# The first layer's adaLN weights: five buffers, and their pool nested inside the norm's

## The chip, the cores and the metric

The kernel runs on one core of a Trainium2 chip. The metric is the device time of one execution in microseconds (us), the median of several runs.

## The reference, cut to what matters

Two layers of a hybrid backbone run over 128 context tokens and 1024 latent tokens, model width 1024, all in float32. Both groups share one set of weights. Each sub-layer is normalised, shifted, scaled and gated by values that come from a conditioning vector (adaLN):

```
mod_p = (silu(c_ctx) @ ada_w[l] + ada_b[l]).reshape(-1, 1, 6, 1024)
mod_s = (silu(c)     @ ada_w[l] + ada_b[l]).reshape(-1, 1, 6, 1024)
hp = modulate(rms_norm(yp, norm_g[l, 0]), mod_p, 0)
hs = modulate(rms_norm(ys, norm_g[l, 0]), mod_s, 0)
# layer 0: even_mixer(h)
q, ff, fb, i, g, hy = split_cols(h @ w_in, (512, 512, 512, 512, 512, 1536))
o_a = bidir_scan(...)                        # HGRN2, 4 heads
hy = dwconv3(hy, hy_conv_w, hy_conv_b);  v, x1, x2 = split(hy, 3)
filt = hyena_filters(L, w1, b1, w2, b2, w3, freq)   # sin, sin, linear, window
z = v
for o, gate in enumerate((x1, x2)):
    z = gate * (two_sided_fftconv(z, filt[o]) + z * hy_d[o])
out = concat([head_rms(o_a) * silu(g), z]) @ w_out
```

After it come a gated ConvFFN, and layer 1 (differential attention and gated linear attention) with another ConvFFN.

## The kernel before

The tokens are nine tiles of 128 rows (one of context, eight latent). A scheduler sets the order of the instructions on each engine ahead of the run: PE (TensorE), DVE (VectorE), ACT (ScalarE), POOL (GpSimd) and SP, which issues nearly all transfers. Each engine works through its order and waits where an instruction's input or buffer is not ready. Every float32 product of the large matrices is three matmuls of a high and a low part (`mm3`, L203 to L207), so each weight is split after its load: the high part on ACT (L211), the low part on DVE or POOL (L218).

What stands at the start of layer 0, in `run`:

- `filter_mlp` (L729): two sine layers over the positions of the Hyena filter; a matmul (L748), seven steps on DVE (L750 to L756), a sine on ACT (L758), three times each layer.
- `ada` (L372), here for group 0, the first four of the twelve blocks of 512 columns: eight loads of 1 MB (`adaw`, L382), four matmuls for each into the PSUM bank tagged `g` (L384), then bias and gain on DVE (L399, L400), four transposes (L408) and copies into `modc`. With `bufs=3` the fourth load waits for the first buffer.
- `first_norm` (L448): for each token tile a load into one of four buffers `y` (L451), square and scale on ACT (L426, L431), and in `to_hT` for each of two half tiles four transposes (L439), the modulation on DVE into one of two buffers `f` (L442), the high part on ACT (L445, `hTh`) and the low part on POOL (L218, `hTl`).
- `filter_tables` (L767) splits the tables of the Fourier transform (`traw`, `tqh`, `tql`), and `columns` (L307) turns small vectors into columns (`rows`, L331, L334, L336).
- `filter_spectra` (L781): the spectra of the filters. The last linear layer's weights are loaded into `X` (L796), summed on POOL (L798) and split (`w3h` on ACT, `w3l` on POOL); matmuls of 256 columns (L812, tag `h`), a window from memory (`win`, L819) multiplied on DVE (L814), a split (`fh` on ACT, `fl` on POOL) and matmuls tagged `f`.
- `hy_in` (L603): the projection of the Hyena columns, twelve blocks of 128 columns, matmuls of 388 columns tagged `g`. Its weights come through `weights` (L225): one load buffer `wraw` (L233) and three each of `whi` and `wlo`, in the pool `gw`.

Then `hyena` (L882), the HGRN projection `hgrn_in` (L645) and the scans of four heads (`hgrn`, L663, `scan`, L485; tags `b` and `c`), beside which the adaLN weights of the other rows are loaded.

Pools on a side of the memory are stacked: a pool opened after others were closed begins where they began, and each tile in it waits until the earlier tiles on its bytes are done. On the left side lie `hT`, then the pools `ada` (weights) and `fn` (norm), and after these two are closed `gw` and `hi` (projection); on the right `keep`, `fm`, and above them first `ml` and `ms` (sine layers) and then `fs` (spectra).

Of the kernel before, what the change touches and what calls it, by code (L numbers as in the profile page):

```python
# [31 lines left out]
def drain(gen):  # L32
    for _ in gen:
        pass
# [160 lines left out]
class Kern:  # L195
# [1273 lines left out]
    def run(self):  # L1469
        L, R = "left", "right"  # L1470
# [4 lines left out]
        with ExitStack() as es:  # L1475
# [6 lines left out]
            with self.psum(g=2, t=2, f=2, h=2):  # L1482
                with self.urgent():
                    self.setup(es)
                self.open_hT(e_hT)
                with self.pool("ada", 1) as ap, self.pool("fn", 2) as np_:
                    with self.pool("ml", 1, R) as mp, self.pool("ms", 2, R) as ms:
                        with self.urgent():
                            self.filter_mlp(keep, mp, ms)
                            drain(self.ada(0, ap, (0,), 3, "g", "t"))  # L1490
                            self.first_norm(np_)
                        self.filter_tables(fp, ms)
                        self.columns()
                    fs = e_keep.enter_context(self.pool("fs", 2, R))
                    drain(self.filter_spectra(fp, fs))
                gw = es_gw.enter_context(self.pool("gw", 3))
                hio = es_hi.enter_context(self.pool("hi", 2))
                drain(self.hy_in(gw, hio, range(4)))
# [58 lines left out]
            with self.psum(b=2, s=4, w=1, ad=1), self.pool("wo", 2) as wo, self.pool("ada", 1) as ad, \  # L1557
# [3 lines left out]
                t = al.tile([P, P], F32, name="p3")  # L1561
# [65 lines left out]
```

## Time and profile before

| | us |
|---|---|
| median of three runs | 3528.32 |
| lowest and highest of the three | 3524.34, 3535.78 |
| the profiled execution | 3525.83 |
| its span, first to last instruction | 3523.8 |

The profile is of one execution. The page gives each engine's busy time and the span in 40 slices; the views of the trace give busy time in chosen stretches, groups of instructions by line, and the instructions in order of time with what ended the idle time before them. PE and PEld are TensorE's matmuls and weight loads; the granted clock is a share of 2.4 GHz.

### The profile page before, as it was taken

The page shows a single profiled execution, that of the slowest core. Times are in us where ns is not written, and L with a number is a line of the kernel's source. Part 1 is how long each engine was busy: PE and PEld are TensorE (multiplying, and loading weights), DVE is VectorE, ACT ScalarE, POOL GpSimd, SP SyncE. Part 2 cuts the span into 40 slices and gives each one's busy share as a digit, 9 for nine tenths or more (in the row PEclk, how much of TensorE's full clock was granted, in tenths as well). Part 3 has the DMA queues.
Part 4 walks back from the last instruction along what each step waited for, and adds up shares of the span by engine and source line. Part 5 has one row for each costly group of instructions (what it writes and reads, how often), then busy time and mean ns, then how long its engine had stood idle before and what let it go on. Part 6 is the DMA issues. An engine that isn't in the chain of part 4 may idle for free.

```text
span 3523.8 us, 55879 instructions
## 1 busy us (share of the span) xinstructions
PE 3334.1 (95%) x23022; PEld 3024.4 (86%) x23022; DVE 1880.8 (53%) x3342; ACT 1354.2 (38%) x2414; POOL 876.4 (25%) x596
## 2 busy tenths in 40 slices
PE   5999999888899999999999999989988999999998
PEld 2999999756699999999988998857767999999997
DVE  5658987488653333433372247558786233343334
ACT  5334333453443222232264334346565322232223
POOL 2432230001442222332240003211125222232214
PEclk7999999999899999999999999989998999999999
DMA  6445334483421110111143323484123110111114
GB/s 217 135 149 151 119 103 136 161 290 123 161 68 48 37 42 25 54 48 43 36 148 119 133 79 115 127 276 108 41 93 104 44 41 26 49 49 48 37 30 138
DMA packets 272701, 348.09 MB, mean 99 GB/s; under 512 B 14354, under 2 KB 231597, under 8 KB 266302
## 3 DMA queue, kind: packets, MB, share of 16 engines
q1 hardware_dynamic: 269294, 334.82, 30.1%
q0 software_dynamic: 3152, 9.70, 0.9%
q8 instruction: 181, 2.97, 0.4%
q14 instruction: 74, 0.61, 0.1%
HBM read 266.58 MB, written 77.89 MB: 98 GB/s over the span
## 4 chain that ended last, share of the span: by engine, by line
PE 79%; DVE 7%; DMA 5%; ACT 3%; issue 3%; POOL 2%; SPq 0%; POOLq 0%; ACTq 0%; DVEq 0%
PE g L206 9%; PE g L207 9%; PE g L205 9%; PE a L205 7%; PE a L206 7%; PE a L207 7%; PE d L205 5%; PE d L206 5%; PE d L207 5%; DMA adaw<-in_ada_w 2%; PE b L1344 1%; PE s L1328 1%; DVE f L442 1%; DVE acc L1002 1%; PE w L205 1%
## 5 line engine op out<-in xcount | busy, mean ns | idle before, releaser
L206 PE MATMUL g<-hTl,whi 128*128 128x388 f32 (+2 forms) x1728 | 589.1, 341 | 2.3 <-POOL hTl L218 2.3
L205 PE MATMUL g<-hTh,whi 128*128 128x388 f32 (+2 forms) x1728 | 588.9, 341 | 2.3 <-ACT hTh L445 2.3
L207 PE MATMUL g<-hTh,wlo 128*128 128x388 f32 (+2 forms) x1728 | 587.6, 341 | 0.0
L206 PE MATMUL a<-hTl,whi 128*128 128x388 f32 (+2 forms) x1248 | 426.7, 342 | 2.6 <-POOL hTl L218 2.6
L205 PE MATMUL a<-hTh,whi 128*128 128x388 f32 (+2 forms) x1248 | 426.9, 342 | 1.4 <-ACT hTh L445 1.4
L207 PE MATMUL a<-hTh,wlo 128*128 128x388 f32 (+2 forms) x1248 | 423.3, 341 | 0.0
L1002 DVE TENSOR_TENSOR acc<-d,acc 128x512 f32<-128x512 f32 x288 | 197.8, 688 | 334.4 <-PE d L207 333.0
L1104 POOL TENSOR_TENSOR ta<-ta,tg 128x386 f32<-128x386 f32 x132 | 135.6, 1027 | 918.2 <-ACT tg L1103 884.0
L205 PEld LDWEIGHTS g<-hTh,whi 128*128 128x128 f32 x1728 | 326.8, 189 | 6.7 <-ACT hTh L445 2.9
L206 PEld LDWEIGHTS g<-hTl,whi 128*128 128x128 f32 x1728 | 326.4, 189 | 6.7 <-POOL hTl L218 2.9
L207 PEld LDWEIGHTS g<-hTh,wlo 128*128 128x128 f32 x1728 | 326.2, 189 | 2.0
L205 PE MATMUL d<-dh,ah 128*128 128x512 f32 x792 | 312.4, 395 | 1.2 <-DVE acc L1002 1.2
L207 PE MATMUL d<-dh,al 128*128 128x512 f32 x792 | 311.8, 394 | 0.0
L206 PE MATMUL d<-dl,ah 128*128 128x512 f32 x792 | 311.7, 394 | 0.0
L476 ACT ACTIVATE tg<-g,cols,cols 128x386 f32<-128x386 f32 x132 | 88.9, 673 | 499.7 <-PE g L207 499.4
L218 POOL TENSOR_TENSOR wlo<-wraw,whi 128x1024 fp32r<-128x1024 f32 x90 | 217.1, 2413 | 165.7 <-ACT whi L211 165.2
L218 POOL TENSOR_TENSOR dl<-draw,dh 128x1024 fp32r<-128x1024 f32 x60 | 147.8, 2464 | 398.8 <-ACT dh L211 327.4
L205 PEld LDWEIGHTS a<-hTh,whi 128*128 128x128 f32 x1248 | 236.5, 189 | 10.2 <-issue 2.2
L206 PEld LDWEIGHTS a<-hTl,whi 128*128 128x128 f32 x1248 | 236.3, 189 | 9.7 <-POOL hTl L218 3.6
L477 DVE SCALAR_TENSOR_TENSOR tg<-g,cols,tg 128x386 f32<-128x386 f32 x132 | 81.8, 620 | 296.6 <-ACT tg L476 296.6
L207 PEld LDWEIGHTS a<-hTh,wlo 128*128 128x128 f32 x1248 | 236.3, 189 | 4.1 <-issue 1.6
L211 ACT ACTIVATE whi<-wraw 128x1024 fp32r<-128x1024 f32 x145 | 152.7, 1053 | 180.0 <-DMA wraw<-in_ffn_up 66.6
(429 smaller groups left out, 7047.7 us busy)
## 6 DMA issues: line engine op xcount, KB each, us to landing
adaw<-in_ada_w SPq DMA_DIRECT2D x48, 1024.0 KB
wraw<-in_ffn_up SPq DMA_DIRECT2D x88, 512.0 KB
draw<-in_ffn_down SPq DMA_DIRECT2D x44, 512.0 KB
wraw<-in_w_in_even SPq DMA_DIRECT2D x32, 512.0 KB
wraw<-in_w_in_odd SPq DMA_DIRECT2D x24, 512.0 KB
hgT<-po SPq DMA_DIRECT2D x16, 576.0 KB
ymid<-acc SPq DMA_DIRECT2D x18, 512.0 KB
y<-ymid SPq DMA_DIRECT2D x18, 512.0 KB
```

Of the source, the lines that this page charges most:

```text
L205: mm(out, lh, rh, start=start, stop=False)
L206: mm(out, lh, rl, start=False, stop=False)
L207: mm(out, ll, rh, start=False, stop=stop)
L211: eng.activation(out, in_, AF.Copy)
L218: eng.tensor_tensor(out, a, b, ALU.subtract)
L442: nc.vector.tensor_scalar(f[:, j], pt[:, 128 * j:128 * j + 128], mod[:, 1, g, k:k + 1], mod[:, 0, g, k:k + 1], ALU.mult, ALU.add)
L476: nc.scalar.activation(out, ps[:, 1:1 + n], AF.Identity, scale=w[1], bias=b)
L477: nc.vector.scalar_tensor_tensor(out, ps[:, 0:n], w[0], out, ALU.mult, ALU.add)
L1002: nc.vector.tensor_tensor(acc[:, i, s], ps, acc[:, i, s], ALU.add)
L1104: nc.gpsimd.tensor_tensor(ta, ta, tg, ALU.mult)
L1328: nc.tensor.matmul(s[:, k0:k0 + 512], q[:, p, 128 * t:128 * t + 128], kx[:, p, k0:k0 + 512], start=(x == 0), stop=(x == 1))
L1344: nc.tensor.matmul(po, w[:, c], v[:, c], start=(c == 0), stop=(c == NT - 1))
```

## The change

The pool `ada` moves inside the block in which `ml` and `ms` are open, and is opened after `fn` in place of before it; it closes before `fs` is opened. The adaLN weights of group 0 get five buffers in place of three.

```diff
-                with self.pool("ada", 1) as ap, self.pool("fn", 2) as np_:
-                    with self.pool("ml", 1, R) as mp, self.pool("ms", 2, R) as ms:
+                with self.pool("fn", 2) as np_:
+                    with self.pool("ada", 1) as ap, self.pool("ml", 1, R) as mp, self.pool("ms", 2, R) as ms:
                         with self.urgent():
                             self.filter_mlp(keep, mp, ms)
-                            drain(self.ada(0, ap, (0,), 3, "g", "t"))
+                            drain(self.ada(0, ap, (0,), 5, "g", "t"))
                             self.first_norm(np_)
                         self.filter_tables(fp, ms)
                         self.columns()
```

The scheduler sets other orders from it. On SP, at the start, the loads before (`adaw` are the adaLN weights, `y` the token tiles, `traw` tables, `rows` small vectors):

```order
L382 DMA adaw<-in_ada_w 128x2048 x3
L451 DMA y<-in_x_prompt 128x1024
L451 DMA y<-in_x_sample 128x1024 x3
L774 DMA traw<-in_const_dft_q 128x1024 x2
L331 DMA rows<-in_hgrn_lb 24x128
L331 DMA rows<-in_hgrn_norm 4x128
L331 DMA rows<-in_hy_conv_w 36x128
L331 DMA rows<-in_hy_conv_b 12x128
L382 DMA adaw<-in_ada_w 128x2048
L394 DMA adab<-in_ada_b 2x512 x3
L396 DMA adag<-in_norm_g 2x512
L394 DMA adab<-in_ada_b 2x512
```

and now:

```order
L382 DMA adaw<-in_ada_w 128x2048 x5
L451 DMA y<-in_x_prompt 128x1024
L451 DMA y<-in_x_sample 128x1024 x3
L774 DMA traw<-in_const_dft_q 128x1024 x2
L331 DMA rows<-in_hgrn_lb 24x128
L331 DMA rows<-in_hgrn_norm 4x128
L382 DMA adaw<-in_ada_w 128x2048
L394 DMA adab<-in_ada_b 2x512 x3
L396 DMA adag<-in_norm_g 2x512
L394 DMA adab<-in_ada_b 2x512
L396 DMA adag<-in_norm_g 2x512
L382 DMA adaw<-in_ada_w 128x2048
```

Two more weight loads go ahead of the token tiles, and the sixth to eighth come ahead of the third and fourth table.

Further on in SP's order, where the projection's weights (`wraw`) are first loaded, before:

```order
L777 DMA traw<-in_const_dft_p 128x256
L331 DMA rows<-in_ffn_conv_w 44x128
L331 DMA rows<-in_ffn_conv_b 44x128
L233 DMA wraw<-in_w_in_even 128x8x128
L451 DMA y<-in_x_sample 128x1024 x2
L233 DMA wraw<-in_w_in_even 128x8x128
L451 DMA y<-in_x_sample 128x1024 x2
L233 DMA wraw<-in_w_in_even 128x8x128
L796 DMA X<-in_hy_w 64x1024 x2
L819 DMA win<-in_const_hy_win 128x2x256
```

and now (`X` are the weights of the spectra, `win` their windows):

```order
L777 DMA traw<-in_const_dft_p 128x256
L331 DMA rows<-in_ffn_conv_b 44x128
L451 DMA y<-in_x_sample 128x1024 x5
L796 DMA X<-in_hy_w 64x1024 x2
L819 DMA win<-in_const_hy_win 128x2x256
L825 DMA at_721<-in_hy_d 1x256
L819 DMA win<-in_const_hy_win 128x2x256 x2
L233 DMA wraw<-in_w_in_even 128x8x128
L825 DMA at_869<-in_hy_d 1x256
L819 DMA win<-in_const_hy_win 128x2x256
```

The first load of projection weights has moved behind the last five token tiles, the spectra's weights and three windows.

On PE, from the transposes of the adaLN rows (L408) to the first projection matmuls (`g<-hTh,whi`), before:

```order
L408 MATMUL t<-ident,adab 128x128
L439 MATMUL t<-ident,y 128x128 x4
L408 MATMUL t<-ident,adab 128x128 x3
L748 MATMUL f<-sh_211,hw_143 64x384
L439 MATMUL t<-ident,y 128x128 x32
L205 MATMUL g<-hTh,whi 128x388
L206 MATMUL g<-hTl,whi 128x388
L207 MATMUL g<-hTh,wlo 128x388
```

and now, first the transposes:

```order
L408 MATMUL t<-ident,adab 128x128
L439 MATMUL t<-ident,y 128x128 x4
L408 MATMUL t<-ident,adab 128x128 x3
L439 MATMUL t<-ident,y 128x128 x4
L748 MATMUL f<-sh_185,hw_143 64x384
L748 MATMUL f<-hz,hw_141 64x384
L439 MATMUL t<-ident,y 128x128 x24
L748 MATMUL f<-sh_211,hw_143 64x384
L439 MATMUL t<-ident,y 128x128 x40
L812 MATMUL h<-w3h,hs 128x256
L812 MATMUL h<-w3h,hs 32x256
```

and then the place where the projection begins:

```order
L205 MATMUL f<-fh,tqh 128x256
L206 MATMUL f<-fl,tqh 128x256
L207 MATMUL f<-fh,tql 128x256
L812 MATMUL h<-w3h,hs 128x256
L812 MATMUL h<-w3l,hs 128x256
L205 MATMUL g<-hTh,whi 128x388
L206 MATMUL g<-hTl,whi 128x388
```

The transposes of the norm (L439) now all stand ahead of the projection, and so do the first matmuls of the spectra (L812 and `f`).

## Rows read from the trace of the kernel before

**Rows 1.** The page, part 2: PE busy in 40 slices of 88 us, in tenths.

```profile
PE   5999999888899999999999999989988999999998
```

**Rows 2.** Stretches: length, busy us (count) of PE, PEld, DVE, ACT, POOL; clock, DMA, GB/s.

```profile
0.00:42.00 42.00, 19.52 (x69) 3.52 (x69) 14.62 (x42) 20.60 (x31) 5.38 (x16) 1.00 0.85 316
42.00:92.00 50.00, 29.32 (x122) 20.53 (x121) 35.67 (x105) 31.66 (x49) 21.71 (x17) 0.62 0.45 122
92.00:350.00 258.00, 256.98 (x1761) 256.13 (x1759) 165.80 (x288) 107.29 (x197) 83.58 (x76) 1.00 0.48 145
681.00:694.00 13.00, 3.91 (x111) 3.27 (x111) 6.75 (x7) 6.17 (x9) 0.00 (x0) 0.61 1.00 342
694.00:840.00 146.00, 131.58 (x1868) 87.22 (x1869) 116.03 (x174) 74.22 (x118) 13.16 (x14) 0.95 0.73 255
840.00:1000.00 160.00, 131.69 (x1004) 107.61 (x1004) 119.40 (x236) 75.90 (x136) 60.30 (x30) 0.86 0.36 117
```

**Rows 3.** Groups by line, PE, 0 to 91.9 us: count, busy us, mean ns, idle.

```profile
L205 PE MATMUL g<-hTh,whi 128*128 128x388 f32 x9 | 4.3, 482 | 2.3 <-ACT hTh L445 2.3
L206 PE MATMUL g<-hTl,whi 128*128 128x388 f32 x8 | 3.9, 490 | 2.3 <-POOL hTl L218 2.3
L207 PE MATMUL g<-hTh,wlo 128*128 128x388 f32 x8 | 3.6, 456 | 0.0
L812 PE MATMUL h<-w3h,hs 128*128 128x256 f32 (+1 forms) x7 | 1.9, 314 | 1.8 <-ACT w3h L211 1.8
L812 PE MATMUL h<-w3l,hs 128*128 128x256 f32 (+1 forms) x7 | 1.9, 317 | 0.0
```

**Rows 4.** In order of time, to 45 us, ACT, PE, SP: start, us, what, idle.

```profile
15.66 1.06 ACT L426 ACTIVATE junk<-y 128x1024 bf16<-128x1024 f32 x1 [12.06 <-DMA y<-in_x_prompt]
25.31 1.94 PE L384 MATMUL g<-adaw,csx 128*32 128x512 f32 x8 [7.44 <-DMA adaw<-in_ada_w]
32.77 1.93 PE L384 MATMUL g<-adaw,csx 128*32 128x512 f32 x8
34.77 0.33 SPq L382 DMA_DIRECT2D adaw<-in_ada_w  x1
42.12 1.89 PE L384 MATMUL g<-adaw,csx 128*32 128x512 f32 x8
```

**Rows 5.** DMA, 0 to 45 us, in 40 slices of 1.1 us: rate.

```profile
GB/s 0 57 154 233 430 394 336 336 323 270 277 397 419 422 422 419 411 429 423 407 269 168 226 430 308 284 422 390 419 452 430 357 204 415 354 98 0 0 0 7
```

**Rows 6.** In order of time, 51 to 101 us, the norm on DVE, ACT, POOL.

```profile
51.58 1.36 DVE L442 TENSOR_SCALAR f<-t,modc 128x128 f32<-128x128 f32 x4
52.98 0.64 ACT L445 ACTIVATE hTh<-f 128x512 fp32r<-128x512 f32 x1 [2.29 <-DVE f L442]
53.77 1.09 POOL L218 TENSOR_TENSOR hTl<-f,hTh 128x512 fp32r<-128x512 f32 x1 [47.20 <-ACT hTh L445]
73.10 1.36 DVE L442 TENSOR_SCALAR f<-t,modc 128x128 f32<-128x128 f32 x4 [0.24 <-POOL hTl L218]
81.91 1.36 DVE L442 TENSOR_SCALAR f<-t,modc 128x128 f32<-128x128 f32 x4 [7.38 <-POOL hTl L218]
98.02 2.64 DVE L442 TENSOR_SCALAR f<-t,modc 128x128 f32<-128x128 f32 x8 [0.36 <-POOL hTl L218]
```

**Rows 7.** In order of time, 63 to 93 us, projection weights and spectra weights.

```profile
63.35 1.04 ACT L211 ACTIVATE whi<-wraw 128x1024 fp32r<-128x1024 f32 x1
71.95 0.69 PE L205 MATMUL g<-hTh,whi 128*128 128x388 f32 x1 [2.27 <-ACT hTh L445]
76.00 1.28 POOL L798 TENSOR_TENSOR X<-X 128x512 f32<-128x512 f32 x1 [2.94 <-DMA X<-in_hy_w]
82.87 2.38 POOL L218 TENSOR_TENSOR w3l<-X,w3h 128x1024 fp32r<-128x1024 f32 x1
92.42 0.34 PE L205 MATMUL g<-hTh,whi 128*128 128x388 f32 x1
92.60 0.34 PE L206 MATMUL g<-hTl,whi 128*128 128x388 f32 x1
```

## The prediction

> **What bounds the kernel now.** I read the page's slices first, then the stretches, then the start in order of time. The only slice in which TensorE (PE) has a digit under 8 is the first [rows 1]: the front is where loads and buffers can matter, and all that follows moves with the moment at which PE is filled for good. The stretches say when that is: 19.5 us of PE work in the first 42 us, 29.3 us in the next 50 us at a mean granted clock of 0.62, then 257.0 of 258 us at full clock [rows 2]. So the front can be put in one number: **the moment at which PE is filled, less the projection and spectra work that it has already done by then**. By 91.9 us it has done 25 matmuls of the first projection (tag g) and 14 of the spectra (tag h) [rows 3]. At full clock one g matmul follows the other after 0.18 us (92.42, 92.60 [rows 7]), so 25 are 4.5 us; an h matmul has 256 columns in place of 388, so some 0.12 us, and 14 are 1.7 us. The front of the kernel before ends, so counted, at 92.0 - 6.2 = 85.8 us. The next stretches with gaps in PE are the scans, 694 to 1000 us: 131.6 of 146 and 131.7 of 160 us busy, with DVE at 116.0 and 119.4 us [rows 2].
>
> **Term 1, five buffers.** With three buffers the eighth weight load is issued at 34.77 us, when the matmuls of the fifth weight, which began at 32.77, have given their buffer back; the last matmuls start at 42.12 [rows 4]. So one buffer wait is real. But the transfers are near their limit anyhow: in the first 42 us the DMA share is 0.85 at a mean of 316 GB/s [rows 2], which is 13.3 MB, and the loads in that stretch (eight weights of 1 MB, four token tiles and four tables of 0.5 MB) are 12.6 MB. Five buffers change the order in which these bytes come, not their number. Two more weights go ahead of the first token tiles, so the prompt rows, whose square starts at 15.66 us [rows 4], come later by 2.1 MB / 316 GB/s, some 6 us. The eighth weight lands after 11.5 MB instead of 12.6, at 3 + 36 = 39 us by the mean rate, and at 3 + 27 = 30 us by the 420 GB/s of the better slices [rows 5]. In the changed order its matmuls stand behind the second sine layer, which waits for the first sine on ACT; and in ACT's order the sine stands behind the scaling of the token tiles, which come 6 us later. So I put the last weight matmuls at 39 to 41 us. From their end, 44.0 us before, DVE needed until 51.58 [rows 4, 6] to modulate the first half tile (L442), with sine steps and table splits in between; these stand there still, more of them. I take 50 for the first L442. Bounds: no gain (51.6), and 6 us of gain, if DVE has done these by then.
>
> The Trainium skill, page "DMA: Bandwidth & Descriptors", section Specifications, puts the HBM limit of one core at some 358 GB/s; by that the eighth weight lands no sooner than 3 + 32 = 35 us. The trace agrees in its mean, 316 GB/s, not in its slices of 1.1 us, which go to 420 GB/s and over [rows 5]. The Trainium skill, page "Perfetto Trace Analysis", section Optimization Strategy, says that the same gap coming again on an engine can mean too few buffers; by that rule PE's waits for the weights would go, which is the second rival below.
>
> **Term 2, the nesting: what the projection's weights lie on.** This is the larger part. Pools on one side are stacked. Before, the adaLN weights' pool stood below the norm's, and the ring of the projection weights (gw), opened when both are closed, began on the adaLN weights, done with at 44 us. Now the norm's pool stands below, so the ring begins on the norm's token buffers and statistics, in use until the ninth token tile is transposed. The orders show it: the first load of projection weights stood on SP ahead of the fifth token tile, and now stands behind all nine, behind the spectra's weights and three windows; on PE all 72 transposes of the norm now stand ahead of the first g matmul. Before, g began at 71.95 [rows 7]. What that costs:
> - The norm's 18 half tiles. The first nine took (73.10 - 51.58) / 8 = 2.7 us each; then DVE stood 7.38 us until POOL, which had waited for the spectra's weights and done their sums and a weight split, gave a buffer free; the last nine, 81.91 to 99.4 us, took 2.2 us each [rows 6, 7]. Now no projection weight is split among them (three on ACT, two on DVE, one on POOL are gone from there), and POOL does fourteen half tiles before the spectra's sums. I take 2.2, of the undisturbed half. Bounds: DVE's own 1.36 [rows 6], which no row comes near, and 2.7.
> - From 50 us the fourteenth half starts at 50 + 13 x 2.2 = 78.6; with DVE 1.36, ACT 0.64 and POOL 1.09 [rows 6] it is out at 81.7. Then POOL: two sums (2 x 1.28), two half tiles (2.2), the low part of the spectra's weights (2.38): 88.8 us, against 82.87 + 2.38 = 85.3 before [rows 7].
> - The first spectra product on DVE, some 0.7 us later, frees a window buffer; behind it SP issues the first projection weights, at some 90.5. Their 0.5 MB need at least 1.7 us at the mean rate, and less than the 7.3 us that 1 MB needed from 34.77 to 42.12 at most [rows 4]; I take 3.7. The split's first half is 1.04 [rows 7]: g starts at some 95.2.
> - By then PE has done some 20 h and 18 f matmuls, 38 x 0.12 = 4.6 us. The front ends at 95.2 - 4.6 = 90.6, against 85.8: **5 us lost**. PE also starts this work from the lower clock level, 1.2 GHz, to which it falls while it only transposes (mean 0.62 of full from 42 to 92 us [rows 2]); before it had risen by 92. That is up to 2 us more, left to the range.
>
> **Term 3, behind the front.** PE's work is the same in sum. The orders differ up to the end of the HGRN scans and are the same behind. One difference has a sign: the spectra now run ahead of the projection, so the Hyena stage and the first scan begin earlier in PE's order. When the first scan's matmuls (tag b) begin, 265 g matmuls are still to come, before 216: 49 x 0.18 = 8.8 us of head start. From 694 us on two scans share DVE, which is busy 0.79 and 0.75 of the time [rows 2]. The scans on the left cannot begin before the last g matmul, because their buffers lie on the projection's inputs, so the gap of 681 to 694, 9.1 us of idle PE [rows 2], stays. What the head start gives is the scan work done before 681. Between nothing and 8.8 us I take **3 us won**, since a scan alone mostly waits for its own chain.
>
> **Sum.** +5 - 3 = +2 us. Against the profiled execution (3525.83 us, its span 3523.8) that is 3527.8; the median of the three runs shown, 3528.32, is 2.5 us above that execution, so I forecast 3530 us. A measurement of this kernel can tell about 0.3%, 10.6 us, from no change: the band is 3517.7 to 3538.9.
>
> **Rivals.**
> 1. *Slower: the half tiles stay at 2.7 us.* The norm's chain through PE, DVE, ACT and POOL with two buffers is then the bound, not the weights' splits between. For it: the first nine took 2.7 with two projection weights among them, and the new ACT order has six changes of its function table in the norm, before three. Against: the last nine took 2.2 beside spectra work. The fourteenth half then starts at 85.1, 6.5 us later, and the projection with it: +11.5; the scans give nothing back if DVE is what they wait for; with a part of the clock's 2 us that is 3528.3 + 13 = 3541. It decides from 2.6 us per half tile on. Chance 0.2.
> 2. *Faster: the buffers do what they are for.* If PE's waits for weights (7.44 us the longest [rows 4]) go and DVE is free when the last one is done, the norm starts at 45.6 in place of 50; with POOL and ACT free of projection weights it runs at 1.9, and 13 halves save 3.9. Then +5 - 4.4 - 3.9 - 3 = -6, and with the whole head start -12: 3516. Against: the DMA share of 0.85. Chance 0.12.
> 3. *The loss is paid back.* The front loses its 5 us, the scans give all 8.8: -4, 3524.5, no difference that can be told. That five buffers do nothing at all, because the bytes set the pace, ends in the forecast or here. Chance 0.13.
>
> **How the numbers follow.** The forecast has 0.55 and lies within the band, rival 3 too: same 0.68. Rival 1 is slower, 0.2; rival 2 faster, 0.12. The range reaches from rival 2 (3516, less 2 for the run-to-run spread) to rival 1 with all of the clock's 2 us and the same spread: 3514 to 3545.
>
> **What would show it.** Right: the last weight matmuls near 40 us and the first L442 near 50; no g matmul before 90 us; POOL without a long stop in the norm; the low part of the spectra's weights done near 88; PE filled from 94 to 96 us on, and the scans' stretch, 306 us before, some us shorter. Wrong: a first L442 before 46, half tiles at 2.7 or under 2, a g matmul before 85, or a change of the scans' stretch of over 8 us either way, which would be an effect of the new order that I have given no price.

## The result and the profile after

The changed kernel takes 3552.7 us (median of four runs, 3548.9 to 3555.6) where the kernel before took 3526.3 in the same session. The ratio is 1.0078, with a 95% interval of 1.0063 to 1.0093: some 26 us slower, and outside the range of the prediction (3514 to 3545). The profiled execution took 3548.93 us, its span 3547.1.

The stretches of the kernel after, as in [rows 2] (length, busy us and count of PE, PEld, DVE, ACT, POOL; granted clock, DMA share, GB/s):

```profile
0.00:42.00 42.00, 20.65 (x74) 3.44 (x74) 11.73 (x42) 19.41 (x28) 5.39 (x16) 0.79 0.84 313
42.00:92.00 50.00, 26.07 (x86) 15.59 (x86) 39.58 (x110) 35.63 (x53) 20.12 (x18) 0.50 0.25 77
92.00:350.00 258.00, 250.90 (x1687) 248.19 (x1686) 156.69 (x269) 103.98 (x188) 84.50 (x75) 0.97 0.49 147
681.00:694.00 13.00, 13.00 (x142) 12.70 (x141) 4.23 (x6) 3.87 (x6) 0.00 (x0) 1.00 0.06 24
694.00:840.00 146.00, 126.61 (x1885) 86.28 (x1884) 110.97 (x160) 75.77 (x125) 15.20 (x17) 0.94 0.78 276
840.00:1000.00 160.00, 129.56 (x1157) 104.91 (x1155) 127.83 (x226) 74.99 (x130) 58.39 (x26) 0.88 0.38 126
```

Between 92 and 350 us PE is 6 us less busy than before, and between 681 and 694 it is still full, where before it stood for 9 of 13 us: the projection and the Hyena stage end 27.6 us later (last g matmul at 706.85, before at 679.23).

To see where these 27.6 us arise, the lag was counted in the way of the prediction: every matmul of the tags g, h, f and y and every transpose of `hy_in` (L619) counts its spacing at full clock (0.18 us for 388 columns, 0.12 for 256), and what the kernel after has done by a moment is subtracted from what the kernel before had done. The count is good to some 1 us.

| by | 92 | 105 | 150 | 225 | 250 | 350 | 400 | 425 | 500 | 550 | 600 |
|---|---|---|---|---|---|---|---|---|---|---|---|
| us behind | 6.4 | 12.5 | 13.5 | 12.6 | 17.4 | 17.1 | 12.0 | 23.3 | 22.8 | 26.7 | 27.1 |

So there are two large losses. **The front loses 13 us**, where I had put 5. **The Hyena stage loses 10 more between 350 and 600 us**, where I had put nothing. Some 4 us arise on the way, at 225 to 250: there PE stands 2.1 us for a window product and 0.4 us for a tile of the projection, and then works at the lower clock level until 232.4 (g matmuls 0.32 us apart in place of 0.18). The scans then give 7.2 back: the first matmul with tag d stands at 927.22 us, 20.4 behind the 906.87 of before. At the first matmul of the projection of layer 1's gated linear attention (`b<-hTh,whi`) it is 19.0 (1909.69, before 1890.67). At the end it is 23.1 in the two profiled executions; from layer 1 on the orders of the two kernels are the same, and what is added there is within what single executions of the kernel before differ by in one session (3516.3 to 3530.8).

The front first, in order of time: the first and last of the lines that answer to [rows 4] and [rows 6], ACT's changes of its function table in the norm, and what leads to the first matmuls of the spectra and the projection (start, us, what, idle before it and its releaser).

```profile
20.56 1.06 ACT L426 ACTIVATE junk<-y 128x1024 bf16<-128x1024 f32 x1 [16.82 <-DMA y<-in_x_prompt]
...
29.52 1.93 PE L384 MATMUL g<-adaw,csx 128*32 128x512 f32 x8 [8.30 <-DMA adaw<-in_ada_w]
...
37.67 1.94 PE L384 MATMUL g<-adaw,csx 128*32 128x512 f32 x8
...
48.06 1.05 DVE L442 TENSOR_SCALAR f<-t,modc 128x128 f32<-128x128 f32 x3
...
59.38 1.28 ACT L758 ACT_TABLE_LOAD   x1
60.67 0.52 ACT L758 ACTIVATE sh<-sa 64x384 f32<-64x384 f32 x1
61.21 1.28 ACT L262 ACT_TABLE_LOAD   x1
...
84.62 2.64 DVE L442 TENSOR_SCALAR f<-t,modc 128x128 f32<-128x128 f32 x8 [1.15 <-POOL hTl L218]
...
87.79 1.26 POOL L798 TENSOR_TENSOR X<-X 128x512 f32<-128x512 f32 x1
89.02 1.27 POOL L218 TENSOR_TENSOR X<-X 128x512 f32<-128x512 f32 x1
...
91.37 2.64 DVE L442 TENSOR_SCALAR f<-t,modc 128x128 f32<-128x128 f32 x8 [2.13 <-POOL hTl L218]
...
92.35 2.34 POOL L218 TENSOR_TENSOR w3l<-X,w3h 128x1024 fp32r<-128x1024 f32 x1
...
95.78 1.01 DVE L814 TENSOR_TENSOR ft<-h,win 128x512 f32<-128x512 f32 x2 [1.78 <-PE h L812]
...
97.29 0.42 SPq L233 DMA_DIRECT2D wraw<-in_w_in_even  x1
...
103.02 0.41 PE L205 MATMUL g<-hTh,whi 128*128 128x388 f32 x1
```

The reader is to see three things. The last weight matmuls stand at 37.67 and the first L442 at 48.06, 3.5 us ahead of before: the buffers gave what was forecast and a little more, although PE still waits 8.30 us for a weight's transfer. The 18 half tiles then need 44.6 us from the start of the first to that of the last (48.06 to 92.7, half of the last row being one half tile), 2.6 us each, and 2.8 up to the fourteenth (84.62), behind which the spectra's sums stand. Sine and square root take turns on ACT: six changes of its table of 1.28 us between 48 and 92 us, three in the kernel before. ACT is busy 29.9 of the 36.6 us up to the fourteenth half tile; in the last nine half tiles of the kernel before, the stretch from which I took 2.2 us, it was busy 7.4 of 17.4 (stretches as in the first table, after and then before):

```profile
48.00:84.60 36.60, 19.42 (x62) 11.17 (x62) 29.00 (x79) 29.92 (x45) 13.81 (x13) 0.50 0.30 94
```

```profile
82.00:99.40 17.40, 15.83 (x96) 14.57 (x97) 15.12 (x42) 7.40 (x12) 13.67 (x12) 0.90 0.27 76
```

And behind the norm stands the chain of Term 2, in its order but late: `w3l` done at 94.7 (before 85.3), the first window product at 95.8, the first projection weights issued at 97.3, g at 103.

The second loss, in the same view (PE, POOL and DVE, 394 to 409 us):

```profile
394.55 0.72 POOL L909 DMA_DIRECT2D kk<-kspec  x1 [3.63 <-DVE Z L892]
398.36 10.49 POOL L218 TENSOR_TENSOR zl<-in,zh 128x256 fp32r<-128x256 f32 x1 [3.08 <-ACT zh L211]
...
407.59 0.67 DVE L892 TENSOR_TENSOR Z<-Z 128x512 f32<-128x512 f32 x1
...
408.90 0.58 PE L206 MATMUL y<-zl,tfh 128*128 128x256 f32 x1 [9.38 <-POOL zl L218]
409.29 0.42 PE L207 MATMUL y<-zh,tfl 128*128 128x256 f32 x1
```

`zl` is the low part of an input of the Hyena transforms (`forward` in `hyena`), a subtraction of 128x256 on POOL that takes 0.73 to 1.54 us where DVE has gaps. Here it took 10.49. DVE worked without a gap from before 385 us to 408.26 (the row at 407.59 is its last), and `zl` ended 0.6 us behind that. PE stood 9.38 us for it, and its first matmuls behind follow each other at 0.21 us in place of 0.12, the lower clock level. The kernel before has the same in a milder form: there `zl` took 7.35 us from 388.16, ending at 395.51 where DVE's run ended at 394.93, and PE stood 4.8 us:

```profile
388.16 7.35 POOL L218 TENSOR_TENSOR zl<-in,zh 128x256 fp32r<-128x256 f32 x1 [2.42 <-ACT zh L211]
394.52 0.41 DVE L914 TENSOR_TENSOR Z<-Z,pt 128x256 f32<-128x256 f32 x1
```

PE's waits for `zl` sum to 9.6 us before and 15.9 after (waits by line, PE, 350 to 560 us, before and then after: sum, number, longest):

```profile
PE y L206 <- POOL zl L218: 9.6, 3, 4.8
```

```profile
PE y L206 <- POOL zl L218: 15.9, 3, 9.4
```

The Trainium skill, page "SBUF — State Buffer", section "Who interferes with whom", says that a DVE operation with two operands in SBUF contends with a GpSimd operation that reads SBUF, and that the loser is fully blocked. The trace agrees, with a number the section does not lead one to expect: the loser was not held for one operation but for the whole run of DVE, some twenty operations of 0.4 to 0.7 us.

### The profile page after: what moved, and what is told of

Its sections match the earlier page's. It is cut to its first block, busy times and chain, and to the rows that moved or that the text cites. A ratio compares the mean times of both kernels' runs of the same rounds, so it can differ in the third digit from the quotient of the medians.

```text
span 3547.1 us, 55887 instructions
## 1 busy us (share of the span) xinstructions
PE 3341.0 (94%) x23022; PEld 3029.1 (85%) x23022; DVE 1894.1 (53%) x3342; ACT 1357.7 (38%) x2417; POOL 883.1 (25%) x596
## 3 DMA queue, kind: packets, MB, share of 16 engines
q1 hardware_dynamic: 269294, 334.82, 29.9%
## 4 chain that ended last, share of the span: by engine, by line
PE 77%; DVE 9%; DMA 5%; issue 3%; ACT 3%; POOL 2%; SPq 0%; POOLq 0%; DVEq 0%; ACTq 0%
PE g L205 8%; PE g L207 8%; PE g L206 8%; PE a L205 7%; PE a L206 7%; PE a L207 7%; PE d L205 5%; PE d L206 5%; PE d L207 5%; DMA adaw<-in_ada_w 2%; PE b L1344 1%; DVE Z L892 1%; PE s L1328 1%; DVE f L442 1%; PE w L205 1%
```

## The experiments

My theory from the two traces: the front's loss is the slow norm (ACT's table changes) together with the ring on the norm's buffers, the second loss is `zl` on POOL in DVE's unbroken runs, and the scans give back some. The rivals: the five buffers and their load order; a DVE that is simply full; POOL's own work for the loads that it issues.

**Three buffers in the new nesting** (e1_nest3):

```diff
-drain(self.ada(0, ap, (0,), 5, "g", "t"))
+drain(self.ada(0, ap, (0,), 3, "g", "t"))
```

> The changed kernel with three buffers in place of five: the nesting alone. Theory (the loss at the front is the nesting, since the projection's ring lies on the norm's buffers; the buffers give some 3 us): first L442 near 51.5 us again, 18 half tiles at about 2.6, no g matmul before 98 us, PE filled from 100 us or later, so that the PE work done by 200 us lags the kernel before by 13 to 17 us; what comes on top behind 250 us depends on this order's own stalls. Time 3540 to 3558. Rival (the five buffers and the load order they bring are the cause): g near 72 us and a time within 6 us of the kernel before.

Measured: 3545.0 us, ratio 1.0064 (1.0049 to 1.0078). First L442 at 51.23, half tiles at 2.6, no g before 103.67, as expected; but the lag at 150 us is 4.5, not 13 to 17. The reason stands on POOL: with three buffers it does the sums of the spectra's weights after seven half tiles, with five after fourteen, and so PE works on the spectra from 77 us (POOL, 73 to 80 us):

```profile
73.20 1.27 POOL L798 TENSOR_TENSOR X<-X 128x512 f32<-128x512 f32 x1 [1.37 <-DMA X<-in_hy_w]
74.43 1.26 POOL L218 TENSOR_TENSOR X<-X 128x512 f32<-128x512 f32 x1
75.65 2.14 POOL L218 TENSOR_TENSOR hTl<-f,hTh 128x512 fp32r<-128x512 f32 x2
77.75 2.35 POOL L218 TENSOR_TENSOR w3l<-X,w3h 128x1024 fp32r<-128x1024 f32 x1
```

So up to 150 us the nesting alone costs the 5 us that I had forecast for the whole change, late g included. Some 5 more arise in it by 225 us, where PE stands 3.5 us for a tile of the projection; all five other kernels with the nested pool lose some 4 us between 150 and 250 us, with 2.3 to 2.7 us of such waits, and those with the pool below the norm's lose nothing there. The other 8 us of the front come with the five buffers, not by their transfers but by the order that the scheduler makes of them. This order has its own stalls behind (9.7 us of waits for `zl`), and here the scans gave nothing back, they took 7 us more.

**Five buffers, the ring on the adaLN weights** (e2_under5): `ada` stays below `fn`, both are closed ahead of the spectra's buffers.

```diff
-with self.pool("fn", 2) as np_:
-    with self.pool("ada", 1) as ap, self.pool("ml", 1, R) as mp, self.pool("ms", 2, R) as ms:
+with self.pool("ada", 1) as ap, self.pool("fn", 2) as np_, self.pool("ml", 1, R) as mp, self.pool("ms", 2, R) as ms:
```

> Five buffers, the pool of the adaLN weights below the norm's as before, both closed ahead of the rings of the spectra, so that the projection's ring lies on the adaLN weights. Theory: first L442 near 48 us, first g matmul at 67 to 72, PE filled by 92 and at full clock there, the work done by 200 us within 0 to 5 us ahead of the kernel before (the spectra's buffers now lie on the norm's last tiles and come later, hidden by projection work). With the Hyena stage as good as before 3520 to 3526, with a stall of POOL's low parts as in the changed kernel up to 3538. Rival (the five buffers and their load order cost the 13 us): the front as late as in the changed kernel, 3545 to 3555.

Measured: 3532.0 us, ratio 1.0026 (1.0016 to 1.0037). The ring is the cause of the late projection: g begins at 70.18 again. What the earlier norm wins is lost at 105 to 110 us, where PE is busy 2.44 of 5 us: the spectra's weights lie on the norm's buffers now, and their sums stand on POOL at 103.91. The lag is 6.2 us at 150 and 2.0 at 600; the time is higher than expected, the rest arising in and behind the scans. With three buffers in this arrangement the order on all engines is that of the kernel before, so the place at which the pool is closed should cost nothing by itself; no run shows it.

**`zl` on DVE, in the kernel after and before** (e3_after_zv, e4_before_zv):

```diff
-self.split(hi, lo, x, nc.scalar, nc.gpsimd)
+self.split(hi, lo, x, nc.scalar, nc.vector)
```

> The changed kernel with the low parts zl of the Hyena transforms computed on DVE in place of POOL. Theory (the second half of the loss is POOL's zl, which gets nowhere while DVE works without a gap: one of them took 10.49 us and PE stood 9.4 us for it, 15.9 us of such waits in all, and some 3 us of work at half clock behind the longest): no PE wait on zl over 1 us between 350 and 560 us, the end of the projection and the Hyena stage 10 to 18 us earlier than in the changed kernel, time 3535 to 3545. The front stays late, so it doesn't come back to 3526. Rival (DVE, busy 0.87 of that stretch, is the limit, and the wait only changes its name): PE waits of the same sum on DVE, time within 4 us of the changed kernel.

> The kernel before with the same edit: zl on DVE. Theory: PE's 9.6 us of waits for zl go, the time falls by 5 to 11 us to 3515 to 3522, less than in the changed kernel, which had 15.9 us of them. Rival (the waits change their name, or the scans give it back): within 3 us of the kernel before.

Measured: 3519.6 us for the changed kernel so edited, ratio 0.9992 (0.9983 to 1.0001) to the kernel before, and 3507.9 for the kernel before so edited, 0.9957 (0.9945 to 0.9970). The stretches 350 to 600 us, first of the changed kernel, then of the same with `zl` on DVE:

```profile
350.00:400.00 50.00, 47.35 (x316) 46.16 (x314) 50.00 (x102) 13.54 (x26) 7.44 (x9) 0.97 0.46 135
400.00:450.00 50.00, 41.10 (x329) 41.10 (x330) 39.94 (x73) 16.95 (x34) 20.63 (x13) 0.90 0.32 101
450.00:600.00 150.00, 143.44 (x868) 142.93 (x867) 133.39 (x251) 48.49 (x98) 32.71 (x25) 0.98 0.37 117
```

```profile
350.00:400.00 50.00, 46.85 (x330) 45.81 (x329) 49.33 (x102) 13.79 (x27) 6.51 (x9) 1.00 0.43 132
400.00:450.00 50.00, 50.00 (x403) 50.00 (x402) 47.68 (x96) 22.40 (x44) 3.62 (x5) 1.00 0.41 122
450.00:600.00 150.00, 150.00 (x919) 149.84 (x919) 134.51 (x269) 51.33 (x104) 10.13 (x14) 1.00 0.39 125
```

PE is full from 400 us on. On DVE the 18 subtractions of this stretch cost 7.5 us in all, 0.41 each, and DVE has room for them. By the medians the edit is worth some 29 us in the changed kernel and 14 in the kernel before, more than I expected of either: besides the waits, the work at the lower clock behind each stall goes (0.90 from 400 to 450 us in the first fence). The front keeps its lag (12.9 us at 150) and the lag at 600 falls from 27.1 to 3.4.

Set against the kernel before with the same edit, the change costs 3519.6 - 3507.9 = 11.7 us. This is not its price without the second loss. At the start of layer 1 the edit is worth 25.2 us in the changed kernel and 24.6 in the kernel before, and the change costs 19.0 us with `zl` on POOL and 18.4 with `zl` on DVE (PE; the kernel before, the changed kernel, then the changed kernel and the kernel before with `zl` on DVE):

```profile
1890.67 0.34 PE L205 MATMUL b<-hTh,whi 128*32 128x386 f32 x1
```

```profile
1909.69 0.34 PE L205 MATMUL b<-hTh,whi 128*32 128x386 f32 x1
```

```profile
1884.50 0.34 PE L205 MATMUL b<-hTh,whi 128*32 128x386 f32 x1
```

```profile
1866.05 0.34 PE L205 MATMUL b<-hTh,whi 128*32 128x386 f32 x1
```

So the stalls of `zl` cost both kernels about the same up to there. At 600 us they make 7.4 of the 27.1 us between the two (19.7 are left with `zl` on DVE), but with `zl` on POOL the scans give these back, and without it they do not. What sets 26.4 and 11.7 us apart (23.3 and 8.1 by the spans of the same executions) arises in layer 1, where the two kernels with `zl` on DVE have other orders than the kernel before and than each other; no run shows how much of it is order and how much the spread of single executions.

**ACT's table changes** (e5_after_nosin). The filter's sines are left out and their arguments passed on, so that the spectra are other values:

```diff
-nc.scalar.activation(o, a, AF.Sin)
+nc.scalar.activation(o, a, AF.Copy)
```

> The changed kernel with the sines of the filter's two layers replaced by plain copies on ACT, so that ACT changes its function table less often; the order on every engine is otherwise that of the changed kernel. Theory (ACT sets the pace of the norm: about 4 us of work per token tile and, in the changed kernel, six changes of its table at 1.28 us among the sines): 18 half tiles at 2.0 to 2.3 us in place of 2.6, the spectra's weights done 5 us earlier, the first window product near 90 in place of 95.8, and the PE work done by 200 us 5 to 7 us more than in the changed kernel; the time 3 to 8 us under the changed kernel, unless the stalls of zl swallow it. Rival (the chain of DVE, ACT and POOL over two buffers sets the pace): half tiles at 2.5 to 2.7, the front as late as in the changed kernel.

Measured: 3541.7 us, 1.0057 (1.0042 to 1.0073), some 6 under the changed kernel, each set against the kernel before in its own session. One table change is left between 48 and 92 us, the half tiles take 2.35 us (47.70 to the last at 87.6), 2.45 up to the fourteenth (79.54), `w3l` is done 5.1 us earlier and the lag at 150 falls from 13.5 to 7.6 (POOL and DVE, 82 to 92 us):

```profile
82.70 1.27 POOL L798 TENSOR_TENSOR X<-X 128x512 f32<-128x512 f32 x1
83.92 1.27 POOL L218 TENSOR_TENSOR X<-X 128x512 f32<-128x512 f32 x1
85.16 2.14 POOL L218 TENSOR_TENSOR hTl<-f,hTh 128x512 fp32r<-128x512 f32 x2
87.26 2.35 POOL L218 TENSOR_TENSOR w3l<-X,w3h 128x1024 fp32r<-128x1024 f32 x1
90.71 0.69 DVE L814 TENSOR_TENSOR ft<-h,win 128x512 f32<-128x512 f32 x1 [1.79 <-PE h L812]
```

So the table changes set a good part of the norm's pace. The remaining 2.35 us is above the 2.3 that I gave as the upper end: something else is not far behind, the chain over two buffers or ACT's other work, which no run tells apart.

**Four buffers** (e6_nest4), the number alone:

> The changed kernel with four buffers in place of five: another order of the same work. Theory (how much the front loses depends on the place of the spectra's weights in POOL's order: five half tiles further back with five buffers than with three; and the stalls behind it on where zl falls into DVE's runs): the front's loss is either some 5 us or some 13, as POOL's order has it, the sum of PE's waits for zl between 5 and 20 us, and the time lies between 3535 and 3555. Rival (the time follows the number of buffers): halfway between the runs with three and five, first L442 at 49 to 50, front loss 8 to 10.

Measured: 3537.6 us, 1.0041 (1.0027 to 1.0055). The lag is 7.2 us at 150 and 13.2 at 600, PE's waits for `zl` are 9.1, first L442 at 48.94. POOL does the sums after nine half tiles, `w3l` is done at 84.8. At the front the rival is nearer: the lag lies between those with three and five buffers, and so does the place of the sums. Time and waits lie in the theory's range, and the time is no mean of the other two but under both, since the scans gave 7 us back here, as with five buffers, and took 7 with three.

**Five buffers below the norm, `zl` on DVE** (e7_under5_zv), both edits from above together:

> Five buffers, the adaLN weights' pool below the norm's, and zl on DVE: the two parts that did not lose, together. Theory: the front as with the ring on the adaLN weights (first g near 70 us), no wait for zl, the end of the projection near 665 us; time 3508 to 3516. If the five buffers are worth their 3.5 us anywhere behind the norm, it beats the kernel before with zl on DVE (3508); I expect that they are not, because the spectra's buffers now lie on the norm's and start late. Rival (the buffers pay once the stalls are gone): 3500 to 3505.

Measured: 3523.1 us, 1.0005 (0.9996 to 1.0014), above the 3508 to 3516 that I expected. The wait for `zl` is gone and the lag at 600 is -8.8 us, but it is not the best of the kernels: the late spectra cost some 7 us against the kernel before with `zl` on DVE (lag 5.8 and -0.9 at 150 us), and the first scan (tag b) stands 8.3 us for ACT. The buffers don't pay here either.

**The loads `kk` issued from SP** (e8_after_kksp in the changed kernel; e9_before_zv_kksp in the kernel before with `zl` on DVE):

```diff
-nc.gpsimd.dma_start(kk, src)
+nc.sync.dma_start(kk, src)
```

> The changed kernel with zl still on POOL, but the 36 loads kk of the filter spectra issued from SP in place of POOL, so that between 350 and 560 us POOL does nothing but zl. Theory (a zl stands still as long as DVE runs operations with two operands in the SBUF memory without a gap): some zl still take 4 to 10 us and end some 0.6 us behind the end of a DVE run, PE's waits for zl stay at 8 us or more in sum; time within 8 us of the changed kernel, the front unchanged. Rival (POOL's own work on the descriptors of the loads it issues is what a zl stands behind): no zl over 2 us, no such wait, 3520 to 3530 as with zl on DVE.

> The kernel before with zl on DVE, and the loads kk issued from SP: nothing is left on POOL in the Hyena stage. Theory: the loads were not what PE waited for, so the end of the projection stays near 661 us and the time within 5 us of 3508. Rival (POOL's late descriptors held up the products): 5 to 10 us less.

Measured: 3535.8 us, 1.0041 (1.0026 to 1.0056), and 3506.4 us, 0.9957 (0.9945 to 0.9970). In the first POOL has nothing but `zl` in this stretch, and three of them still take over 5 us. The longest, and DVE's last operations beside it:

```profile
398.71 6.21 POOL L218 TENSOR_TENSOR zl<-in,zh 128x256 fp32r<-128x256 f32 x1 [65.63 <-ACT zh L211]
```

```profile
403.60 0.42 DVE L913 TENSOR_TENSOR Z<-Z,pt 128x256 f32<-128x256 f32 x1
403.93 0.42 DVE L914 TENSOR_TENSOR Z<-Z,pt 128x256 f32<-128x256 f32 x1
407.03 0.69 DVE L218 TENSOR_TENSOR gl<-Z,gh 128x512 fp32r<-128x512 f32 x1 [2.68 <-ACT gh L211]
```

`zl` ends at 404.92, 0.6 us behind the end of DVE's run at 404.35. POOL had issued nothing for 65 us, so its descriptors are not what `zl` stood behind. My sizes were off, though: in this order PE's waits for `zl` sum to 6.4 us and not 8 or more, and the time fell by some 13 us, 5 of them by the start of layer 1. A blocked `zl` need not reach PE whole: the longest of these waits is 2.2 us, behind a `zl` of over 5. The second kernel is as fast as the one with `zl` alone on DVE: these loads were on no path. The two are the fastest kernels of the study, 14 to 16 us under the kernel before.

All of it in one table. The lag is against the kernel before, in us; d is the first matmul with tag d, 906.87 us before; layer 1 is the first matmul `b<-hTh,whi`, 1890.67 us before; the time is the median less that of the kernel before in the same session.

| kernel | lag 150 | lag 600 | d | layer 1 | time |
|---|---|---|---|---|---|
| after | 13.5 | 27.1 | +20.4 | +19.0 | +26.4 |
| after, 3 buffers | 4.5 | 9.4 | +18.7 | +18.0 | +22.7 |
| after, 4 buffers | 7.2 | 13.2 | +6.3 | +7.1 | +16.0 |
| after, no sines | 7.6 | 22.2 | +15.3 | +14.4 | +20.1 |
| after, kk from SP | 14.1 | 16.6 | +15.6 | +14.2 | +13.2 |
| after, zl on DVE | 12.9 | 3.4 | -1.6 | -6.2 | -2.7 |
| 5 buffers, ada below | 6.2 | 2.0 | +3.2 | +4.5 | +9.7 |
| 5 buffers, ada below, zl on DVE | 5.8 | -8.8 | -10.5 | -11.6 | +1.5 |
| before, zl on DVE | -0.9 | -16.3 | -22.7 | -24.6 | -14.4 |
| before, zl on DVE, kk from SP | -0.3 | -14.9 | -21.5 | -23.6 | -16.3 |

All columns but the last are of one execution each, the times of several, so that the last column differs from that before it by up to 13 us. Only the kernels after with four and five buffers and without sines have the orders of the kernel before in layer 1; the others differ there too.

## Why the prediction was wrong

- **Term 1, five buffers: right.** Last weight matmuls at 37.7 to 39.6 (39 to 41 forecast), first L442 at 48.06 (50 forecast, 45.6 to 51.6 the bounds). PE's waits for the weights sum to 16.4 us, 14.7 before: the transfers remained the limit, and rival 2 fell.
- **Term 2, the nesting: right in its chain, wrong in a size.** The ring on the norm's buffers, the spectra ahead of the projection, POOL's and SP's orders came as described, and e2_under5 shows the ring as the cause of the late g. What failed first is the step "I take 2.2, of the undisturbed half". Up to the fourteenth the half tiles took 2.8 us, over the pace of rival 1. The 2.2 came from a stretch in which ACT was busy 7.4 of 17.4 us, since nearly all token tiles had been scaled by then; ahead of the fourteenth half tile ACT had that work still to do, and six table changes in place of three, which I had written down. e5_after_nosin shows the table changes at work: without five of them it is 2.45 us. That the scaling on ACT makes up the rest is argued and not shown. With the forecast start at 50 the fourteenth half was to be out at 81.7; the sums began at 87.8, although the start was 2 us earlier. In the forecast's own sum: the first projection weights were issued at 97.3 in place of 90.5, g began at 103.0 in place of 95.2, and PE had done 33 spectra matmuls by then in place of 38, at 0.12 us 4.0 in place of 4.6 us. So the front ended at 99.0 and not at 90.6, 13.2 us behind the 85.8 of before, where I had 5. The clock, "up to 2 us more", was the second size: from 92 to 105 us PE was busy 9.9 us for some 6 us of work at full clock. These 4 us lie inside the 13 and do not come on top.
- **"PE's work is the same in sum. ... One difference has a sign": this step let the order behind the front pass at no cost.** At the first d the parts are 13 at the front, 4 at 225 to 250, 10 in the Hyena stage and 7 given back by the scans, 20 us where I had 2. So 8 of the 18 us are Term 2's, 14 had no term, and the scans took 4 of them back. 7.4 of the 10 in the Hyena stage are stalls of `zl`, which the kernel before has too: it gains 24.6 us up to layer 1 and 14 in the median without them. They are not what made the change slow up to there, since without them it costs 18.4 us at layer 1 in place of 19.0. I had not read PE's waits behind 350 us, because PE's digits there are 9s, and 5 us in a slice of 88 do not change a digit. The text named "an effect of the new order that I have given no price" as what would make it wrong. The last 7 us, from 19.0 at layer 1 to 26.4 in the medians, stay open.
- **Term 3, the scans: right sign, low size, by a wrong reason.** 7.2 us came back against the 3 forecast. Half of them are in the gap ahead of the left scans, which I had said would stay (PE idle 10.9 of the 15.1 us from 679.3 before, 7.4 of the 15.1 us from 706.9 after). And the head start does not decide it. With three buffers the first scan's first matmul stands 62.7 us ahead of the last g, more than the 53.6 in the changed kernel, and the scans' stretch is 7 us longer than before instead of 7 shorter. Between the two kernels with `zl` on DVE the scans give nothing back (20.8 us at the last g, 21.1 at the first d). What decides stays open.
- **The rivals.** Rival 1, at a chance of 0.2, had the front nearly right: the fourteenth half tile at 85.1 (84.62 came) and 11.5 us lost, with a part of the clock's 2. It named the table changes; how far the chain over two buffers, its other reason, counts is not shown. Its 3541 lacked what arose behind the front. The range ended at 3545 because no case of mine had a loss behind the front.

The exact share of POOL's order in the front stays open too. With `w3l` done at 80.1, 84.8, 89.6 and 94.7 us the lag is 4.5, 7.2, 7.6 and 13.5, but no run moves the sums alone.

## What to carry to other kernels

Before pricing a change that makes a scheduler order everything anew, look through the whole trace for operations whose duration varies tenfold (here one of 0.73 to 10.49 us): such a stall is a lottery that any new order draws again (PE's waits for it sum to 6.2 to 16.5 us in the seven kernels with `zl` on POOL), and taking it away was worth 14 us, more than the best case I had given the change (12). And compare two kernels at a point up to which the same work is done, not only at the end: here the medians alone would have laid 15 us on a cause that both kernels share. More buffers for a load only help if what is stacked on their place can still start; say which later pool lies on which earlier one. Where one engine serves two chains that need different function tables, count the changes in the new order and take the slower pace if they double.

## What the runs showed of the hardware

A POOL subtraction of two SBUF operands does not share with a DVE that runs operations of two SBUF operands back to back; it waits for DVE's next gap. The twelve of over 6 us in the seven kernels with `zl` on POOL (6.07 to 10.49 us) all ended 0.6 us behind the end of the DVE run. A DVE operation with one operand in PSUM lets it through as a gap does. In the changed kernel one of 5.41 us ended at 456.41 although DVE worked on; the operation at 455.75 reads `y` from PSUM, and the same stands in three other kernels, 0.66 us from the start of that operation to the end of `zl` each time:

```profile
451.01 5.41 POOL L218 TENSOR_TENSOR zl<-in,zh 128x256 fp32r<-128x256 f32 x1 [4.09 <-ACT zh L211]
```

```profile
455.75 0.41 DVE L968 TENSOR_TENSOR in<-y,in 128x256 f32<-128x256 f32 x1
456.09 0.88 DVE L894 SCALAR_TENSOR_TENSOR Z<-Z 128x512 f32<-128x512 f32 x1
```

The granted clock of the profile can be missing a fall. In the run of the changed kernel with `zl` on DVE, whose front is the same, the clock of 42 to 103 us reads 1.00, where it reads 0.50 to 0.51 in the changed kernel. Yet the norm's transposes take 433 ns in both, and the h matmuls are as slow: 456 and 471 ns, against 312 in the kernel before (groups by line, PE, 55 to 105 us; first the changed kernel, then the one with `zl` on DVE).

```profile
L812 PE MATMUL h<-w3h,hs 128*128 128x256 f32 x9 | 4.2, 471 | 1.6 <-ACT w3h L211 1.0 <-DVE ft L814 0.6
```

```profile
L812 PE MATMUL h<-w3h,hs 128*128 128x256 f32 x9 | 4.1, 456 | 1.7 <-ACT w3h L211 1.0 <-DVE ft L814 0.6
```

The durations, not the column, tell the level there.
